# Layer 0 of a two-layer encoder: values of four head pairs by rows of tokens of a class, and eight reads of the head factors in place of sixteen

## The chip, the cores and the metric

The kernel runs on one core of one Trainium2 chip. The core has a matrix engine (TensorE, in the profile PE, its weight loads PEld), a vector engine (VectorE, DVE), a scalar engine (ScalarE, ACT), a general engine (GpSimd, POOL) and a queue engine (SyncE, SP) that issues nearly all DMAs here. Each engine works through its own instructions strictly in the order in which the program lists them; semaphores hold an instruction until what it needs is done.

The metric is the device time of one execution in microseconds (us). The kernel before takes 1204.83 us, the median of three runs from 1204.46 to 1208.03.

## The reference

One sequence of 512 tokens with 1024 features goes through two layers, each a token mixer and a squared-ReLU MLP with RMSNorm ahead of both. Layer 0, which the change touches, mixes by dilated sliding windows over 16 heads of 64 features:

```
A_GROUPS = ((128, 1, 6), (512, 4, 5), (2048, 16, 5))     # window, dilation, heads
qkv = xn @ w_qkv
...
lse = logsumexp(logits); p = exp(logits - lse); o = p @ v_sel
glses.append(logsumexp(lse over the group's heads) - log(nh))
alpha = softmax(stack(glses))                             # over the three groups
out = concat([o_g * (3 * alpha_g)]) @ w_o
```

Heads 0 to 5 look at 129 neighbours. Heads 6 to 15 look only at tokens whose number leaves the same remainder modulo 4, so for them the 512 tokens fall into four classes of 128 and a class attends to itself alone. Each head's output is scaled, token by token, by a factor that needs the sums of the softmax of all heads: 1 over the head's own sum times its group's weight.

## The kernel before, in words

**Layout and precision.** Activations lie turned: features on the 128 partitions, tokens along the free dimension, eight tiles of 128x512 for 1024 features. Every product of weights is made from a rounded part and a rest of both operands, three matmuls for each block of 128 features (helper `mm3`, lines 168 to 170 of the profile: high by high, high by low, low by high). The weights are the stationary operand and 512 tokens stream past. Weights come in units of 1 MB from a list (`units`), fetched one unit ahead into two buffers (`raw`, L154), rounded on ScalarE (`whi`, L157) and subtracted on VectorE (`wlo`, L158), each in two pieces. A unit's DMA can be issued only when the subtraction two units earlier has released the buffer.

**Layer 0's mixer.** Heads go in pairs (64 + 64 features make one tile of 128 partitions). For a pair: logits (L505), a bias and a minimum on VectorE (L485), exponentials and their sums on ScalarE (L487, two buffers `psg`), four transposes on TensorE (L538), a copy to SBUF on VectorE (L539). Then `values0(j)` makes the values of pairs 2j and 2j+1: 24 matmuls a pair, a multiplication by the norm's factor with the tokens sorted by class on VectorE (L550, `v`), four transposes on TensorE (L553), a copy on ScalarE (L555, `vn`), eight products with the probabilities (L565, into `o_ps`; the profile counts two records for each) and a copy (L567, `o`).

**The head factors.** `group_stats` sums the softmax sums by group. The sums of heads 6 to 15 are held by class, those of heads 0 to 5 by token, so each goes to DRAM and back in the other order: `exS` (L631) and `allN` (L632). `head_factors` makes the factors (`sA`, last step L602), `factors` turns them on TensorE (L642), copies them (`fT`, L644) and writes them to DRAM (`fac`, L645); heads 6 to 15 go first, heads 0 to 5 need `allN`. `spread` reads them back, each row repeated over 64 partitions (`fB`, L652): two DMAs for a pair of heads, sixteen in all.

**The output projection.** For each pair, in the order of `HEADS`, VectorE multiplies outputs and factors (L670), ScalarE rounds (`oh`, L678) and VectorE subtracts (`ol`, L679). Then eight tiles of 128 output features are made from four units of `a_w_o`, 24 matmuls for a tile, so 192 in all, and added to the residual `h` (L684).

**What sets the order.** A scheduler orders every engine's instructions when the program is built, from its own estimates. The code can move it with `high_priority` and with `issue_after`, which keeps what follows behind a named instruction. On the chip the order is fixed.

Of the kernel before, what the change touches and what calls it, by code (L numbers as in the profile page):

```python
# [11 lines left out]
F32 = mybir.dt.float32  # L12
# [70 lines left out]
def tile_encoder(ctx: ExitStack, tc: tile.TileContext, x, rel_bias, gains, norm_final_g,  # L83
# [15 lines left out]
    def acc_tile():  # L99
        return ps_acc.tile([P, 512], F32, tag="acc", name="acc")  # L100

    def s_tile():
        return ps_s.tile([P, 512], F32, tag="s", name="s_ps")
# [39 lines left out]
    def unit(w, r0, kt, c0, nc_):  # L143
        units.append((w, r0, kt, c0, nc_))
# [22 lines left out]
    def mm3(ps, ahi, alo, bhi, blo, first, last):  # L167
        nc.tensor.matmul(ps, ahi, bhi, start=first, stop=False)  # L168
        nc.tensor.matmul(ps, ahi, blo, start=False, stop=False)  # L169
        nc.tensor.matmul(ps, alo, bhi, start=False, stop=last)  # L170

    def linear_steps(ct0, kt, ncol, xs, on_out, bank=None, hooks=(), hold=None, order=None):

# [99 lines left out]
    def qkv_unit(w, part, j):  # L273
        unit(w, 0, KT, part * DM + j * 256, 256)
# [9 lines left out]
                    unit(mlp_w_out[i], c * 1024 + q * 512, 4, 0, 512)  # L284

    MLP_ORDER = [("in", 0), ("in", 1), ("out", 0), ("in", 2), ("out", 1), ("in", 3), ("out", 2), ("out", 3)]
    for part, j in ((0, 0), (1, 0), (0, 1), (1, 1), (2, 0), (0, 2), (1, 2), (2, 1), (0, 3), (1, 3), (2, 2), (2, 3)):
        qkv_unit(a_w_qkv, part, j)
    for c in range(4):
        unit(a_w_o, 0, KT, c * 256, 256)  # L290
    mlp_units(0)
# [101 lines left out]
    def lam():  # L393

        lam4 = spool.tile([P, 4, 64], F32, tag="nsq", name="lam4")
        nc.sync.dma_start(lam4.rearrange("p a b -> p (a b)"),
                          b_lambda.rearrange("a b -> (a b)").unsqueeze(0).broadcast_to([P, 256]))
        lprod = spool.tile([P, 2, 64], F32, tag="nsq", name="lprod")
        lsum = const.tile([P, 2], F32, name="lsum")
        nc.vector.tensor_mul(lprod, lam4[:, 0::2, :], lam4[:, 1::2, :])  # L400
        nc.vector.tensor_reduce(lsum, lprod, axis=AX.X, op=ALU.add)
        nc.scalar.activation(lsum, lsum, AF.Exp)
        nc.vector.tensor_sub(nlam, lsum[:, 1:2], lsum[:, 0:1])
        nc.vector.tensor_scalar(nlam, nlam, -LAMBDA_INIT, None, op0=ALU.add)
# [137 lines left out]
    def values0(j):  # L542
# [26 lines left out]

        run(linear_steps(2 * j, KT, 256, norm.xs, out_v))  # L570

    allN = l0p.tile([P, NB, 3, 2], F32, name="allN", bufs=1)
    allS = l0p.tile([P, NB, 3, 2], F32, name="allS", bufs=1)
    exN = dram.tile([SEQ, 2], F32, name="exN")
# [12 lines left out]
    def head_factors(al, parts):  # L587

        M = l0p.tile([P, NB, 1], F32, tag="fM", name="fM")
        nc.vector.tensor_reduce(M, al[:, :, :, 0], axis=AX.X, op=ALU.min)  # L590
        e = l0p.tile([P, NB, 3], F32, tag="fe", name="fe")
        nc.vector.tensor_sub(e, al[:, :, :, 0], M.broadcast_to([P, NB, 3]))
        nc.scalar.activation(e, e, AF.Exp, scale=-1.0)
        nc.vector.tensor_mul(e, e, al[:, :, :, 1])
        W = l0p.tile([P, NB, 1], F32, tag="fW", name="fW")
        nc.vector.tensor_reduce(W, e, axis=AX.X, op=ALU.add)
        nc.vector.reciprocal(W, W)
        nc.vector.tensor_scalar(W, W, 3.0, None, op0=ALU.mult)
        nc.vector.tensor_mul(e, e, W.broadcast_to([P, NB, 3]))
        for s, lo, hi, g in parts:  # L600
            nc.vector.reciprocal(s[:, :, lo:hi], s[:, :, lo:hi])
            nc.vector.tensor_mul(s[:, :, lo:hi], s[:, :, lo:hi], e[:, :, g:g + 1].broadcast_to([P, NB, hi - lo]))  # L602
# [11 lines left out]
        hankel(B1[:, 5:10, :], 11, 5, E_G2, P)  # L614
    values0(0)
    lam()
    probs0(2)
    probs0(3)
    group_stats(allN[:, :, 0, :], mnN, sN, 6)
# [18 lines left out]
    def factors(h0, h1):  # L638
        n = (h1 - h0) * NB
        with tc.high_priority():  # L640
            T = t_tile()
            nc.tensor.transpose(T[0:n, 0:P], sA[:, h0:h1, :].rearrange("p h b -> p (h b)"), ident)  # L642
            fT = l0p.tile([40, P], F32, tag="fT", name="fT")
            nc.scalar.copy(fT[0:n], T[0:n, 0:P])  # L644
        nc.sync.dma_start(fac[h0 * NB:h1 * NB], fT[0:n])  # L645

    def spread(*pairs):
        f = l0p.tile([P, 2, SEQ], F32, tag="ptn", name="fB", bufs=4)
        for i, p in enumerate(pairs):
            for hh, rows in enumerate((lo64, hi64)):  # L650
                a = fac[0:1, 0:1]
                nc.sync.dma_start(f[rows, i, :], bass.AP(tensor=a.tensor, offset=a.offset + (2 * p + hh) * SEQ,  # L652
                                                         ap=[[0, 64], [1, SEQ]]))
            F[p] = f[:, i, :]

    head_factors(allS, [(sS, 0, 5, 1), (sS, 5, 10, 2)])
    factors(6, 16)
    spread(3, 4)
    head_factors(allN, [(sN, 0, 6, 0)])
    factors(0, 6)  # L660
    spread(5, 0)
    spread(1, 2)
    spread(6, 7)
    values0(2)
    values0(3)

    oh_, ol_ = {}, {}
    HEADS = (3, 4, 5, 0, 1, 2, 6, 7)
    for p in HEADS:
        nc.vector.tensor_mul(F[p], O[p], F[p])  # L670
        hi = hpool.tile([P, SEQ], F32R, tag=f"Bh{p}", name=f"oh{p}")
# [15 lines left out]

    nm = Norm(G_MLP0, "A")
    on = residual(nm)
    for c in range(4):  # L690
        run(linear_steps(2 * c, KT, 256, (oh_, ol_), on, bank=wide, order=HEADS))
    l0.close()
    qk.close()
# [374 lines left out]
```

## Time and profile before

| | |
|---|---|
| median of the runs | 1204.83 us |
| profiled execution, its own time | 1205.12 us |
| its span | 1203.1 us |
| TensorE busy | 1186.0 us, 99% of the span |
| weight loads busy | 992.1 us, 82% |
| VectorE busy | 628.2 us, 52% |
| ScalarE busy | 501.1 us, 42% |
| GpSimd busy | 82.0 us, 7% |
| mean granted TensorE clock | 0.997 of full speed |

Times within the profile are us from the start of the span. The stage that the change touches runs from about 152 us (the first value product of pair 4) to 234 us (the last addition of the output projection). A row of the timeline gives start, length, engine, line, operation, what is written and read, and in brackets the idle time ahead of it with what ended it. TensorE's records overlap: a matmul of 512 columns is shown with 0.39 us while the next one starts 0.23 us after it.

### The profile page before, as it was taken

The page shows a single profiled execution, that of the slowest core. Times are in us where ns is not written, and L with a number is a line of the kernel's source. Part 1 is how long each engine was busy: PE and PEld are TensorE (multiplying, and loading weights), DVE is VectorE, ACT ScalarE, POOL GpSimd, SP SyncE. Part 2 cuts the span into 40 slices and gives each one's busy share as a digit, 9 for nine tenths or more (in the row PEclk, how much of TensorE's full clock was granted, in tenths as well). Part 3 has the DMA queues.
Part 4 walks back from the last instruction along what each step waited for, and adds up shares of the span by engine and source line. Part 5 has one row for each costly group of instructions (what it writes and reads, how often), then busy time and mean ns, then how long its engine had stood idle before and what let it go on. Part 6 is the DMA issues. An engine that isn't in the chain of part 4 may idle for free.

```text
span 1203.1 us, 14799 instructions
## 1 busy us (share of the span) xinstructions
PE 1186.0 (99%) x5888; PEld 992.1 (82%) x5888; DVE 628.2 (52%) x1056; ACT 501.1 (42%) x924; POOL 82.0 (7%) x141
## 2 busy tenths in 40 slices
PE   8999999999999999999999999999999999999997
PEld 6888877888888888888888898987888888888887
DVE  5875467544434334425458868675644344334323
ACT  6663345443323313313357666664443134223233
POOL 0000000200000000001101221222200000000012
PEclk9999999999999999999999999999999999999999
DMA  7622223323323332233423323312323332333211
GB/s 226 143 83 71 71 92 99 113 84 105 105 77 99 105 105 87 89 105 105 127 94 102 101 82 101 117 51 83 97 83 105 105 102 76 103 105 105 77 64 70
DMA packets 106827, 117.82 MB, mean 98 GB/s; under 512 B 5014, under 2 KB 97366, under 8 KB 106710
## 3 DMA queue, kind: packets, MB, share of 16 engines
q1 hardware_dynamic: 106694, 116.61, 30.7%
q8 instruction: 46, 0.75, 0.3%
q0 software_dynamic: 64, 0.27, 0.1%
q14 instruction: 23, 0.18, 0.0%
HBM read 114.60 MB, written 2.27 MB: 97 GB/s over the span
## 4 chain that ended last, share of the span: by engine, by line
PE 95%; DMA 2%; DVE 1%; issue 1%; SPq 0%; ACT 0%; POOLq 0%; POOL 0%; DVEq 0%; ACTq 0%
PE acc L169 15%; PE acc L168 15%; PE acc L170 15%; PE s_ps L168 14%; PE s_ps L170 14%; PE s_ps L169 14%; PE o_ps L915 2%; PE s_ps L358 1%; PE s_ps L359 1%; PE t_ps L906 1%; PE o_ps L565 1%; PE s_ps L505 0%; PE t_ps L527 0%; DMA fac<-fT 0%; DMA raw<-in_a_w_qkv_dram 0%
## 5 line engine op out<-in xcount | busy, mean ns | idle before, releaser
L157 ACT CAST whi<-raw 128x1024 fp32r<-128x1024 f32 (+1 forms) x196 | 189.1, 1014 | 385.6 <-PE s_ps L169 205.3
L158 DVE TENSOR_TENSOR wlo<-raw,whi 128x1024 fp32r<-128x1024 f32 (+1 forms) x196 | 223.4, 1180 | 38.4 <-ACT whi L157 37.9
L168 PE MATMUL acc<-Ah,whi 128*128 128x512 f32 x472 | 185.6, 393 | 0.0
L170 PE MATMUL acc<-Ah,wlo 128*128 128x512 f32 x472 | 185.5, 393 | 0.0
L169 PE MATMUL acc<-Al,whi 128*128 128x512 f32 x472 | 184.8, 392 | 0.0
L168 PE MATMUL s_ps<-Ah,whi 128*128 128x512 f32 x352 | 137.7, 393 | 0.6 <-ACT whi L330 0.6
L169 PE MATMUL s_ps<-Al,whi 128*128 128x512 f32 x352 | 137.3, 392 | 0.0
L170 PE MATMUL s_ps<-Ah,wlo 128*128 128x512 f32 x352 | 136.9, 392 | 0.0
L170 PEld LDWEIGHTS acc<-Ah,wlo 128*128 128x128 f32 x472 | 88.8, 188 | 18.4
L169 PEld LDWEIGHTS acc<-Al,whi 128*128 128x128 f32 x472 | 88.8, 188 | 18.1
L168 PEld LDWEIGHTS acc<-Ah,whi 128*128 128x128 f32 x472 | 88.8, 188 | 17.7
L713 ACT ACTIVATE u<-u 128x512 f32<-128x512 f32 x64 | 40.0, 628 | 96.6 <-DVE u L712 96.6
L168 PEld LDWEIGHTS s_ps<-Ah,whi 128*128 128x128 f32 x352 | 66.3, 189 | 16.3 <-ACT whi L330 1.4
L722 DVE TENSOR_TENSOR h<-h,s_ps 128x512 f32<-128x512 f32 x33 | 22.7, 688 | 108.0 <-PE s_ps L170 108.0
L170 PEld LDWEIGHTS s_ps<-Ah,wlo 128*128 128x128 f32 x352 | 66.5, 189 | 13.8
L169 PEld LDWEIGHTS s_ps<-Al,whi 128*128 128x128 f32 x352 | 66.5, 189 | 13.7
L712 DVE SCALAR_TENSOR_TENSOR u<-s_ps,rB 128x512 f32<-128x512 f32 x38 | 26.3, 691 | 76.0 <-PE s_ps L170 73.8
L245 POOL TENSOR_TENSOR nacc<-nacc,nsq 128x512 f32<-128x512 f32 x18 | 25.9, 1438 | 534.2 <-ACT nsq L243 533.7
L168 PE MATMUL s_ps<-Bh,whi 128*128 128x512 f32 x152 | 59.1, 389 | 0.0
L169 PE MATMUL s_ps<-Bl,whi 128*128 128x512 f32 x152 | 59.1, 389 | 0.0
L170 PE MATMUL s_ps<-Bh,wlo 128*128 128x512 f32 x152 | 59.1, 389 | 0.0
L887 DVE CUSTOM_DVE_ANT_0 p<-s_ps,bias 128x512 f32<-128x512 f32 x64 | 43.3, 688 | 26.3 <-PE s_ps L359 17.7
(246 smaller groups left out, 2148.2 us busy)
## 6 DMA issues: line engine op xcount, KB each, us to landing
raw<-in_mlp_w_in_dram SPq DMA_DIRECT2D x32, 1024.0 KB, 5.3
raw<-in_mlp_w_out_dram SPq DMA_DIRECT2D x32, 1024.0 KB, 5.2
raw<-in_b_w_qkv_dram SPq DMA_DIRECT2D x12, 1024.0 KB, 5.2
raw<-in_a_w_qkv_dram SPq DMA_DIRECT2D x10, 1024.0 KB, 6.6
bias<-fd SPq DMA_DIRECT2D x16, 448.0 KB, 3.4
raw<-in_a_w_o_dram SPq DMA_DIRECT2D x4, 1024.0 KB, 5.2
raw<-in_b_w_o_dram SPq DMA_DIRECT2D x4, 1024.0 KB, 6.3
h<-in_x_dram SPq DMA_DIRECT2D x8, 256.0 KB, 4.4
```

The source lines that it names most:

```text
L157: nc.scalar.copy(hi[:, :, c], raw[:, :, c])
L158: nc.vector.tensor_sub(lo[:, :, c], raw[:, :, c], f32(hi[:, :, c]))
L168: nc.tensor.matmul(ps, ahi, bhi, start=first, stop=False)
L169: nc.tensor.matmul(ps, ahi, blo, start=False, stop=False)
L170: nc.tensor.matmul(ps, alo, bhi, start=False, stop=last)
L245: eng.tensor_add(self.acc, self.acc, sq)
L358: nc.tensor.matmul(S, q[m][:, qs], k[m][:, ks], start=True, stop=False)
L712: nc.vector.scalar_tensor_tensor(u, ps, 0.0, nm.rB, op0=ALU.max, op1=ALU.mult)
L713: nc.scalar.activation(u, u, AF.Square)
L722: nc.vector.tensor_add(hT[ct], hT[ct], ps)
L887: nc.vector.tensor_tensor_reduce(out=xt, in0=S, in1=bias[h][m][:, b * P:b * P + SEQ], scale=1.0, scalar=3.0e38, op0=ALU.add, op1=ALU.min, ...
L915: marks["PV"] = nc.tensor.matmul(O[:, b, :], aT[:, k, :], v[:, k, es], start=k == 0, stop=k == NB - 1)
```

## The change

**Values.** Pairs 0 to 3 are done as before. For pairs 4 to 7 a new function `values_by_class` takes `values0(2)` and `values0(3)`'s place. The normalised activations are now the stationary operand, for each class the 128 tokens of it, that is every fourth column of the tile, and the weights of the four pairs (512 columns) stream past. So the values come with tokens on the partitions, one PSUM bank for each class, and need no transposes. The norm's factor is then one number for each partition; it is written to DRAM and read back by class once, early (`exR`, `rC`), and applied by ScalarE when it copies a bank (`vc`). The weights come as two units of 512 features by 512 columns. The matmuls of one half of the features run over all four banks, then those of the other half. The eight products of a pair with the probabilities are as many as before; they go to `o_ps` and `t_ps` banks in turn.

**Factors.** `spread` reads the factors of two pairs with one DMA for each half of the partitions, 64 x 2 x 512 elements in place of 64 x 512; eight DMAs move what sixteen moved. The pairs go together as (3,4), (6,7), (0,1), (2,5).

**Order.** The fourth bank of the first half is kept behind the turning of the factors of heads 6 to 15, the second bank of the second half behind that of heads 0 to 5. `HEADS` runs from 0 to 7. The first unit of the projection is written out with its two tiles going side by side, pair by pair.

```diff
-    for part, j in ((0, 0), (1, 0), (0, 1), (1, 1), (2, 0), (0, 2), (1, 2), (2, 1), (0, 3), (1, 3), (2, 2), (2, 3)):
+    for part, j in ((0, 0), (1, 0), (0, 1), (1, 1), (2, 0), (0, 2), (1, 2), (2, 1), (0, 3), (1, 3)):
         qkv_unit(a_w_qkv, part, j)
+    for half in range(2):
+        unit(a_w_qkv, half * 512, 4, 2 * DM + 512, 512)
...
+    exR = dram.tile([SEQ, 1], F32, name="exR")
+    rC = l0p.tile([P, NB, 1], F32, name="rC", bufs=1)
+
+    def values_by_class(behind):
+        xh, xl = norm.xs
+        v = [qkp.tile([P, SEQ], F32, tag=tag, name="vc", bufs=3) for tag in ("q0", "k0", "q0", "k0")]
+        banks = [acc_tile(), acc_tile(), s_tile(), s_tile()]
+        mark = None
+        for half in range(2):
+            hi, lo = next_w()
+            for c, ps in enumerate(banks):
+                mark = behind.get((half, c), mark)
+                with tc.issue_after(mark.ins) if mark else nullcontext():
+                    for k in range(4):
+                        d = 4 * half + k
+                        ah, al = (t.rearrange("p (m c) -> p c m", c=4)[:, c, :] for t in (xh[d], xl[d]))
+                        mm3(ps, ah, al, hi[:, k, :], lo[:, k, :], d == 0, d == KT - 1)
+                if half == 1:
+                    nc.scalar.activation(v[c], ps, AF.Copy, scale=rC[:, c, :])
+        for p in range(4, 8):
+            ops = (o_tile, t_tile, t_tile, o_tile)[p - 4]()
+            for b in range(NB):
+                for hh, rows in enumerate((lo64, hi64)):
+                    e = (p - 4) * P + 64 * hh
+                    nc.tensor.matmul(ops[rows, b * P:(b + 1) * P], v[3 - b][:, e:e + 64], PT[2 * p + hh][:, b, :],
+                                     start=True, stop=True)
+            o = hpool.tile([P, SEQ], F32, tag=f"Bl{p}", name=f"o{p}")
+            nc.scalar.copy(o, ops)
+            O[p] = o
...
     lam()
+    nc.sync.dma_start(exR.rearrange("(q p) s -> p q s", p=P), norm.r.unsqueeze(2))
+    nc.sync.dma_start(rC, exR.rearrange("(m c) s -> m c s", c=4))
...
-    def spread(*pairs):
+    def spread(p0, p1):
         f = l0p.tile([P, 2, SEQ], F32, tag="ptn", name="fB", bufs=4)
-        for i, p in enumerate(pairs):
-            for hh, rows in enumerate((lo64, hi64)):
-                a = fac[0:1, 0:1]
-                nc.sync.dma_start(f[rows, i, :], bass.AP(tensor=a.tensor, offset=a.offset + (2 * p + hh) * SEQ,
-                                                         ap=[[0, 64], [1, SEQ]]))
-            F[p] = f[:, i, :]
+        for hh, rows in enumerate((lo64, hi64)):
+            a = fac[0:1, 0:1]
+            nc.sync.dma_start(f[rows], bass.AP(tensor=a.tensor, offset=a.offset + (2 * p0 + hh) * SEQ,
+                                               ap=[[0, 64], [2 * (p1 - p0) * SEQ, 2], [1, SEQ]]))
+        F[p0], F[p1] = f[:, 0, :], f[:, 1, :]
...
-    factors(6, 16)
+    turned_s = factors(6, 16)
     spread(3, 4)
+    spread(6, 7)
     head_factors(allN, [(sN, 0, 6, 0)])
-    factors(0, 6)
-    spread(5, 0)
-    spread(1, 2)
-    spread(6, 7)
-    values0(2)
-    values0(3)
+    turned_n = factors(0, 6)
+    spread(0, 1)
+    spread(2, 5)
+    values_by_class({(0, 3): turned_s, (1, 1): turned_n})
...
-    HEADS = (3, 4, 5, 0, 1, 2, 6, 7)
+    HEADS = (0, 1, 2, 3, 4, 5, 6, 7)
...
-    for c in range(4):
+    hi, lo = next_w()
+    banks = [wide(), wide()]
+    for p in HEADS:
+        for c, ps in enumerate(banks):
+            s = slice(c * P, (c + 1) * P)
+            mm3(ps, hi[:, p, s], lo[:, p, s], oh_[p], ol_[p], p == HEADS[0], p == HEADS[-1])
+    for c, ps in enumerate(banks):
+        on(c, ps)
+    for c in range(1, 4):
         run(linear_steps(2 * c, KT, 256, (oh_, ol_), on, bank=wide, order=HEADS))
```

**How it moves instructions.** Line numbers in the changed kernel are higher: the turning of the factors is L679 there (L642 before), the write of `fac` L682 (L645), the read of `fB` L690 (L652), the products with the probabilities L601 (L565), the multiplication by the factors L707 (L670), the subtraction for `ol` L716 (L679).

On SP, around the factors, before:

```order
L154 DMA raw<-in_a_w_o_dram 128x8x256 x2
L631 DMA exS<-allS 512x1x4
L632 DMA allN<-exS 128x4x4
L154 DMA raw<-in_a_w_o_dram 128x8x256
L645 DMA fac<-fT 40x128
L645 DMA fac<-fT 24x128
L652 DMA fB<-fac 64x512 x16
L154 DMA raw<-in_a_w_o_dram 128x8x256
```

and in the changed kernel:

```order
L154 DMA raw<-in_a_w_o_dram 128x8x256 x2
L668 DMA exS<-allS 512x1x4
L669 DMA allN<-exS 128x4x4
L682 DMA fac<-fT 40x128
L690 DMA fB<-fac 64x2x512 x4
L682 DMA fac<-fT 24x128
L154 DMA raw<-in_a_w_o_dram 128x8x256
L690 DMA fB<-fac 64x2x512 x4
L154 DMA raw<-in_a_w_o_dram 128x8x256
```

The third unit of `a_w_o` stood ahead of both writes of `fac`; now it stands behind them and ahead of the last four reads, which bring the factors of pairs 0, 1, 2 and 5.

On VectorE, behind the factors of heads 0 to 5 (`o_1229`, `o_803`, `o_857` and `o_1184` are the outputs of pairs 3, 0, 1 and 2, `o_1757` that of pair 4; `ol_1794` belongs to pair 0, `ol_1799` to pair 1), in the changed kernel:

```order
L637 TENSOR_TENSOR sA<-sA,fe 128x4x6
L707 TENSOR_TENSOR fB<-o_1229,fB 128x512
L158 TENSOR_TENSOR wlo<-raw,whi 128x8x128 x2
L707 TENSOR_TENSOR fB<-o_803,fB 128x512
L707 TENSOR_TENSOR fB<-o_857,fB 128x512
L707 TENSOR_TENSOR fB<-o_1184,fB 128x512
L158 TENSOR_TENSOR wlo<-raw,whi 128x8x128 x2
L716 TENSOR_TENSOR ol_1794<-fB,oh_1793 128x512
L707 TENSOR_TENSOR fB<-o_1757,fB 128x512
L716 TENSOR_TENSOR ol_1799<-fB,oh_1798 128x512
```

Before, the subtractions for `v` stood among these, and only one unit's `wlo` stood here, behind six of the eight multiplications. Now the first unit's `wlo`, whose end lets SP issue the third unit, stands behind the multiplication of pair 3, and the second unit's stands ahead of the first `ol`.

On TensorE, around the first turning of factors, in the changed kernel (`wlo` and `whi` now stream; the `s_ps` below L679 is the fourth bank):

```order
L168 MATMUL s_ps<-whi,Ah_122 128x512
L169 MATMUL s_ps<-wlo,Ah_122 128x512
L170 MATMUL s_ps<-whi,Al_130 128x512
L540 MATMUL t_ps<-ident,psg 128x128 x4
L679 MATMUL t_ps<-ident,sA 40x128
L168 MATMUL s_ps<-whi,Ah_119 128x512
L169 MATMUL s_ps<-wlo,Ah_119 128x512
```

Before, this turning stood 68 value products into the stage; now it stands 36 in, and the second one (24x128) 60 in.

More of the change, by code (lines that the diff above doesn't have):

```diff
@@ L169, in mm3 @@
         nc.tensor.matmul(ps, ahi, blo, start=False, stop=False)
-        nc.tensor.matmul(ps, alo, bhi, start=False, stop=last)
+        return nc.tensor.matmul(ps, alo, bhi, start=False, stop=last)
     def linear_steps(ct0, kt, ncol, xs, on_out, bank=None, hooks=(), hold=None, order=None):
@@ L641, in factors @@
             T = t_tile()
-            nc.tensor.transpose(T[0:n, 0:P], sA[:, h0:h1, :].rearrange("p h b -> p (h b)"), ident)
+            mark = nc.tensor.transpose(T[0:n, 0:P], sA[:, h0:h1, :].rearrange("p h b -> p (h b)"), ident)
             fT = l0p.tile([40, P], F32, tag="fT", name="fT")
@@ L645, in factors @@
         nc.sync.dma_start(fac[h0 * NB:h1 * NB], fT[0:n])
-    def spread(*pairs):
+        return mark
+    def spread(p0, p1):
         f = l0p.tile([P, 2, SEQ], F32, tag="ptn", name="fB", bufs=4)
-        for i, p in enumerate(pairs):
-            for hh, rows in enumerate((lo64, hi64)):
-                a = fac[0:1, 0:1]
-                nc.sync.dma_start(f[rows, i, :], bass.AP(tensor=a.tensor, offset=a.offset + (2 * p + hh) * SEQ,
-                                                         ap=[[0, 64], [1, SEQ]]))
-            F[p] = f[:, i, :]
+        for hh, rows in enumerate((lo64, hi64)):
[3 more added lines that the diff above has]
+        F[p0], F[p1] = f[:, 0, :], f[:, 1, :]
     head_factors(allS, [(sS, 0, 5, 1), (sS, 5, 10, 2)])
-    factors(6, 16)
+    turned_s = factors(6, 16)
     spread(3, 4)
+    spread(6, 7)
     head_factors(allN, [(sN, 0, 6, 0)])
-    factors(0, 6)
-    spread(5, 0)
-    spread(1, 2)
-    spread(6, 7)
-    values0(2)
-    values0(3)
+    turned_n = factors(0, 6)
+    spread(0, 1)
+    spread(2, 5)
+    values_by_class({(0, 3): turned_s, (1, 1): turned_n})
     oh_, ol_ = {}, {}
-    HEADS = (3, 4, 5, 0, 1, 2, 6, 7)
+    HEADS = (0, 1, 2, 3, 4, 5, 6, 7)
     for p in HEADS:
```

## The prediction

> **What bounds the kernel now.** I read the page first: its busy shares and the chain that ended last.
>
> ```profile
> PE 1186.0 (99%) x5888; PEld 992.1 (82%) x5888; DVE 628.2 (52%) x1056; ACT 501.1 (42%) x924; POOL 82.0 (7%) x141
> PE 95%; DMA 2%; DVE 1%; issue 1%; SPq 0%; ACT 0%; POOLq 0%; POOL 0%; DVEq 0%; ACTq 0%
> ```
>
> TensorE is the bound, and what it can still save is work taken off it or a hole closed. The chain's 2% of DMA is worth a look: for a while something other than TensorE ends last. The timeline of TensorE in the stage that changes shows where:
>
> ```profile
> 151.86 0.39 PE L168 MATMUL acc<-Ah,whi 128*128 128x512 f32 x1
> 152.09 0.40 PE L169 MATMUL acc<-Al,whi 128*128 128x512 f32 x1
> ...
> 157.45 1.16 PE L505 MATMUL s_ps<-k,q 64*128 64x128 f32 x16
> ...
> 172.58 0.27 PE L642 MATMUL t_ps<-ident,sA 128*24 128x128 f32 x1 [0.92 <-DVE sA L602]
> 172.68 0.60 PE L553 MATMUL t_ps<-ident,v 128*128 128x128 f32 x4
> 173.96 1.09 PE L565 MATMUL o_ps<-pt,vn 128*64 128x128 f32 x16 [0.68 <-ACT vn L555]
> ...
> 180.60 1.09 PE L565 MATMUL o_ps<-pt,vn 128*64 128x128 f32 x16
> 181.62 0.66 PE L553 MATMUL t_ps<-ident,v 128*128 128x128 f32 x4
> 182.04 0.48 PE L169 MATMUL acc<-Al,whi 128*128 128x512 f32 x1
> ...
> 183.40 0.50 PE L168 MATMUL s_ps<-oh,whi 128*128 128x512 f32 x1 [0.65 <-ACT oh L678]
> ...
> 186.33 1.12 PE L553 MATMUL t_ps<-ident,v 128*128 128x128 f32 x4 [2.20 <-DVE v L550]
> 187.38 1.98 PE L565 MATMUL o_ps<-pt,vn 128*64 128x128 f32 x16
> ...
> 189.68 0.40 PE L169 MATMUL s_ps<-ol,whi 128*128 128x512 f32 x1
> ```
>
> Four holes in brackets, 4.45 us. Behind the last one the same work is slower (1.98 us against 1.09 for eight products, 1.12 against 0.66 for four transposes): the granted clock was halved there.
>
> ```profile
> 186.00:189.40 3.40, 3.07 (x21) 2.41 (x21) 3.40 (x6) 2.76 (x5) 0.00 (x0) 0.50 0.42 131
> ```
>
> That is another 1.35 us. And each set of four transposes of `v` holds the stream 0.42 us (181.62 to 182.04) to 0.6, four sets together 2.0. So the old scheme costs at most 7.8 us.
>
> **What the change takes away.** The 16 transposes, 2.0 us. Also the four copies `vn` and VectorE's four multiplications `v`, and with them the two holes that name them (0.68 and 2.20). The value products stay 96 of 512 columns, the products with the probabilities 32, the projection 192: moved, at one price.
>
> **The strided weight load.** A weight load now takes every fourth column. No stationary operand of before is so spread, so I bound it. These are matmuls of 256 columns in layer 1, and the cast to `oh`, whose output has a step of four elements for pairs 3 to 7 and of one for pairs 0 to 2.
>
> ```profile
> 695.56 0.28 PE L168 MATMUL acc<-whi,Ah 128*128 128x256 f32 x1
> 695.67 0.28 PE L169 MATMUL acc<-wlo,Ah 128*128 128x256 f32 x1
> 695.79 0.28 PE L170 MATMUL acc<-whi,Al 128*128 128x256 f32 x1
> L170 PEld LDWEIGHTS acc<-Ah,wlo 128*128 128x128 f32 x472 | 88.8, 188 | 18.4
> L678 ACT CAST oh<-fB x8: 618/1144/1183, 182.2 to 195.8; 128x512 fp32r<-128x512 f32 x8
> ```
>
> Loads of 128 columns follow each other every 0.12 us there, so one occupies its path 0.12 us at most, though its record has 188 ns. Under a 512-column matmul (0.23 us from start to start) it has 0.11 us to spare. ScalarE pays 1183/618 = 1.9 times for the step of four. 1.9 x 0.12 = 0.23 us: just hidden. Lower bound nothing; upper bound 1.9 times the whole record, 0.36 us, or 0.13 us more for each of 96 products. I take nothing, as the nearest row for a load's pace is the 256-column one.
>
> [...] By an estimate with a factor of 2 on the 0.12 us, 0.24, the sum would change by less than 1 us; a larger factor is the second rival.
>
> **The chain that takes over.** With the transposes gone, what TensorE waits for next are the factors. SP's timeline and the landing times (for the write `exS`, for `fB`, for a weight unit `raw`):
>
> ```profile
> 164.30 0.59 SPq L631 DMA_DIRECT2D exS<-allS  x1
> 167.71 0.37 SPq L632 DMA_DIRECT2D allN<-exS  x1
> 170.87 0.37 SPq L154 DMA_DIRECT2D raw<-in_a_w_o_dram  x1
> 171.34 2.12 SPq L645 DMA_DIRECT2D fac<-fT  x2
> 176.27 10.33 SPq L652 DMA_DIRECT2D fB<-fac  x16
> DMA to landing us min/median/max: 3.4/3.4/3.4
> DMA to landing us min/median/max: 2.8/3.0/3.5
> DMA to landing us min/median/max: 5.0/5.2/5.4
> L652 SPq DMA_DIRECT2D fB<-fac x16: 449/590/599, 176.3 to 186.0; - x16
> ```
>
> and VectorE's rows that the steps below use:
>
> ```profile
> 164.17 0.11 DVE L585 TENSOR_SCALAR allS<-gsz 128x4 f32<-128x4 f32 x1
> 164.91 0.69 DVE L539 COPY pt<-t_ps 128x512 f32<-128x512 f32 x1
> 165.92 0.29 DVE L602 TENSOR_TENSOR sA<-sA,fe 128x20 f32<-128x20 f32 x2
> 169.54 0.17 DVE L590 TENSOR_REDUCE fM<-allN 128x4 f32<-128x12 f32 x1 [1.26 <-DMA allN<-exS]
> 169.62 1.22 DVE L158 TENSOR_TENSOR wlo<-raw,whi 128x1024 fp32r<-128x1024 f32 x1
> 172.23 0.20 DVE L602 TENSOR_TENSOR sA<-sA,fe 128x24 f32<-128x24 f32 x1
> L670 DVE TENSOR_TENSOR fB<-o,fB x8: 674/694/701, 179.8 to 195.1; 128x512 f32<-128x512 f32 x8
> L679 DVE TENSOR_TENSOR ol<-fB,oh x8: 672/1115/1149, 186.7 to 197.0; 128x512 fp32r<-128x512 f32 x8
> 188.91 2.37 DVE L158 TENSOR_TENSOR wlo<-raw,whi 128x1024 fp32r<-128x1024 f32 x2
> ```
>
> Now step by step, on the clock of before.
>
> 1. The last logits stand 12 products into the stage, not 23, so 2.5 us earlier (151.86 + 12 x 0.23 + two transposes, 154.8). Little of it arrives: the last head's exponentials wait for one of two `psg` buffers, which the transposes of the head before it free between value products (about 160.9), and VectorE copies the last turned head (0.69) ahead of the last sum. I get `exS` issued at 164.0, before 164.3.
> 2. The factors of heads 6 to 15 need 1.4 us more (164.17 to 166.2, less the copy): 165.4. TensorE is at their turning after 36 products, 163.0. **New hole, 2.4 us**, and every value product behind it waits. The second turning stands 24 products later, 171.0; its factors come at 171.2, since the `wlo` of 1.22 us is gone from between 169.54 and 172.23. Hole 0.2.
> 3. TensorE ends the value products at 179.3, waits for the last bank's copy (the hole of 0.68 for `vn` again, 0.75), and makes three sets of products, 3 x 1.02, to 183.2. Next stands the first product with `oh` of pair 0.
> 4. When is that there? `exS` lands at 164.0 + 3.4 = 167.4; SP issues the read of `allN` and at 167.8 `fac`. No weight unit stands ahead of that write; before, one issued 0.47 us ahead of it did, and the first `fB` came 4.9 us after `fac`. I take 3.0 (bounds 1.8, from 167.71 to 169.54, and 4.9): 170.8. Four `fB` at 0.59 each; the first two, with twice the data (1 MB takes 2.2 us more than 128 KB, so 0.3), land by 174.8.
> 5. VectorE multiplies pair 3 (0.69), then subtracts the first unit (2.37): 177.9. Only then can SP issue the third unit, and the reads for pairs 0, 1, 2 and 5 are queued behind it. 177.9 + 5.2 = 183.1 for the unit, then four reads of 256 KB at 0.6: pair 0 and 1 at 184.4, pair 2 and 5 at 185.6.
> 6. `oh` of pair 0 is ready at 184.4 + 0.69 + 0.62 = 185.7. **Hole 2.5 us.** Four products and the last set of eight take TensorE to 187.7.
> 7. `ol` of pair 0 stands on VectorE behind the multiplications of pairs 0 to 2 (to 186.3) and the second unit's subtraction (2.37): 188.7 + 0.67 = 189.4. **Hole 1.8 us**; TensorE goes on at 189.5. From there VectorE needs 1.8 us for a pair (0.69 + 1.12) against 2.7 for its twelve products, so nothing more waits.
>
> **The sum.** At 189.5 four of the 192 projection products and all others are done. Before, at 189.68, three were done and one set of eight, 1.02 us, still to come. So the change is ahead by 0.2 + 0.23 + 1.0 = **1.4 us**. Beyond that both have the same products, and before ran them without a hole to the last addition:
>
> ```profile
> 233.97 0.69 DVE L684 TENSOR_TENSOR h<-h,s_ps 128x512 f32<-128x512 f32 x1 [3.21 <-PE s_ps L170]
> ```
>
> (189.68 + 189 x 0.227 + 1.02 = 233.6; 0.23 is the step of the rows above, 0.227 the mean that fits this run.) Counted the other way, 7.8 of old cost less new holes of 2.4 + 0.2 + 0.75 + 2.5 + 1.8 = 7.65 leaves 0.15 ahead; the list of old costs misses what a switch between kinds of products loses without a hole. I take the sum by times and keep 1 us of doubt. The two early DMAs for `rC` move SP's weight loads of that stage by about a microsecond; TensorE waits for none there. If that cover were gone it would cost that microsecond.
>
> The profiled execution took 1205.12 us (span 1203.1, 2.0 around it), 0.3 above the median of 1204.83. So: 1204.83 - 1.4 = **1203.4 us**, within 0.3% (3.6 us), which is about what a measurement of this kernel tells from no change.
>
> **Rivals.** *The chain does not gate: faster.* If the reads of step 5 come early (a quicker `fac`, or reads that pass the weight unit), holes 6 and 7 close and TensorE is through at 185.2 in place of 189.5: 4.3 us more, 1199.1 us. For it: every step is a landing time that I carried over. Against: the order of SP and VectorE is fixed, and `fac` before waited just as I assume. Chance 0.23.
>
> *The strided load is not hidden: slower.* At 0.36 us for each value product the 36 ahead of step 2 cost 4.7 us, which the chain of the factors carries along, and the 60 others 7.8. TensorE then ends the values at 191.8 and reaches the state of step 7 at 197.5 in place of 189.5: 8.0 less 1.4, 1211.4 us. It decides from 0.04 us more for a product: 36 x 0.04 = 1.4, the whole gain. For it: the cast's 1.9. Against: 0.11 us to spare. [...] Chance 0.17.
>
> *The half clock comes back behind a new hole.* Before, the holes of 0.65 and 2.20 within 3.6 us brought it; steps 6 and 7 leave 2.5 and 1.8 within 6.3, step 2 has 2.4. It would cost up to 1.7 us, after 189.5 only, since before that TensorE waits anyway: 1205.1, still no change.
>
> That eight reads are not half of sixteen is certain: each moves twice the bytes; the queue saves eight issues of 0.59 us, which are hidden behind step 5's unit.
>
> **Numbers.** Chain gates, 0.60 (half clock included): 1203.4, by itself 1201.5 to 1206. Not gating 0.23, load not hidden 0.17. Range 1199.3 to 1208.0: it takes in most of the first rival and the middle of the second. Faster by over 0.3%: 0.24; within: 0.59; slower: 0.17.
>
> **What would show it.** Right: a hole of 2 us or more ahead of the first turning of factors, two more between the third and the last set of products and the first `ol`, `fB` of pair 0 landing after the third unit of `a_w_o`, and 0.23 us between value products. Wrong: value products at over 0.25 us; no hole after the third set of products; or a hole beyond 190 us, where VectorE would be the bound.

## The result and the profile after

The changed kernel is slower: 1215.07 us median (1213.41 to 1216.91) against 1205.76 us of the kernel before on the same chip. The ratio is 1.0082, with a 95% interval of 1.0069 to 1.0095. The profiled execution has a span of 1211.3 us against 1203.1, so 8.2 us are to be found between the two traces.

I looked first at two marks that both kernels have: the last set of logits but one, ahead of the stage that was changed, and the last row shown in the prediction, an addition to `h` at the end of that stage (233.97 us before). Of before, and then of the changed kernel:

```profile
150.43 1.16 PE L505 MATMUL s_ps<-k,q 64*128 64x128 f32 x16
```

```profile
157.64 1.16 PE L507 MATMUL s_ps<-k,q 64*128 64x128 f32 x16
...
242.25 0.69 DVE L721 TENSOR_TENSOR h<-h,s_ps 128x512 f32<-128x512 f32 x1 [3.21 <-PE s_ps L170]
```

7.21 us are lost before the stage of the values begins, where no instruction of TensorE was changed. The stage itself takes 84.61 us in place of 83.54, another 1.07. So the question is what happens ahead of 150 us, and there the change puts only the two small DMAs for `rC`. SP's timeline, of before:

```profile
31.78 0.88 SPq L434 DMA_DIRECT2D B<-fd  x2
37.08 0.37 SPq L154 DMA_DIRECT2D raw<-in_a_w_qkv_dram  x1
...
40.73 39.20 SPq L154 DMA_DIRECT2D raw<-in_a_w_qkv_dram  x4
```

The same place in the changed kernel:

```profile
30.79 0.88 SPq L436 DMA_DIRECT2D B<-fd  x2
32.37 0.36 SPq L652 DMA_DIRECT2D exR<-rstd  x1
43.59 0.34 SPq L653 DMA_DIRECT2D rC<-exR  x1
44.05 0.37 SPq L154 DMA_DIRECT2D raw<-in_a_w_qkv_dram  x1
...
47.55 39.57 SPq L154 DMA_DIRECT2D raw<-in_a_w_qkv_dram  x4
```

and the row on it in the list of SP's waits, whose columns are the sum in us, how often, and the longest:

```profile
SPq L653 <- DMA exR<-rstd: 10.8, 1, 10.8
```

Issuing the two takes 0.7 us. But the second one reads what the first one writes, so SP holds it until `exR` has landed, 10.8 us, and everything behind it in SP's order is held too. The weight unit goes out at 44.05 in place of 37.08, and the next one at 47.55 in place of 40.73. That next one lands 19.5 us after its issue (19.7 before), so it is late by about as much as it was issued late. ScalarE's cast of it, in the kernel before, with the exponentials that follow:

```profile
60.52 2.00 ACT L157 CAST whi<-raw 128x1024 fp32r<-128x1024 f32 x2 [0.81 <-DMA raw<-in_a_w_qkv_dram]
...
64.49 0.51 ACT L487 ACTIVATE PN<-xt,mnN 128x256 f32<-128x256 f32 x1
```

and in the changed kernel, with what stands behind it on ScalarE and then on TensorE:

```profile
67.13 1.99 ACT L157 CAST whi<-raw 128x1024 fp32r<-128x1024 f32 x2 [8.00 <-DMA raw<-in_a_w_qkv_dram]
...
71.07 0.51 ACT L489 ACTIVATE PN<-xt,mnN 128x256 f32<-128x256 f32 x1
...
71.72 1.13 PE L529 MATMUL t_ps<-ident,PN 128*128 128x128 f32 x4 [7.30 <-ACT PN L489]
```

The stretch behind that, with the busy time of each engine and then the granted clock (0.54):

```profile
72.00:76.00 4.00, 4.00 (x14) 3.19 (x14) 3.84 (x15) 3.47 (x15) 0.00 (x0) 0.54 0.74 249
```

ScalarE stands 8 us before a cast whose data are not there. Three more casts and then the exponentials `PN` are queued behind it, and TensorE waits 7.30 us for those. When it goes on, the clock is halved for most of 4 us. In the kernel before, the same four transposes wait for nothing:

```profile
66.40 0.60 PE L527 MATMUL t_ps<-ident,PN 128*128 128x128 f32 x4
```

71.72 - 66.40 = 5.3 us of the 7.21 are their delay, and the half clock accounts for most of the rest. The cast is 6.6 us late and the transposes only 5.3, because before, the exponentials had been ready 1.3 us ahead of TensorE: that was all the cover there was. The hole is longer than the delay, because this execution came to it 2 us ahead. It was ahead by that much already where SP writes `fd` (27.00 us against 29.14), in front of anything that the change touches; of the kernels below, some write it at 27 us and some at 29. TensorE's wait names ScalarE; only ScalarE's own wait names the DMA, and only SP's wait tells why that DMA was late.

In the stage of the values the holes are where they were looked for (TensorE's timeline of the changed kernel):

```profile
173.94 0.27 PE L679 MATMUL t_ps<-ident,sA 128*40 128x128 f32 x1 [2.30 <-DVE sA L637]
...
190.99 1.09 PE L601 MATMUL o_ps<-pt,vc 128*64 128x128 f32 x16 [0.78 <-ACT vc L595]
...
195.31 0.50 PE L168 MATMUL s_ps<-oh,whi 128*128 128x512 f32 x1 [1.48 <-ACT oh L715]
...
199.30 0.50 PE L169 MATMUL s_ps<-ol,whi 128*128 128x512 f32 x1 [1.77 <-DVE ol L716]
```

and the clock behind the first of them is 0.50:

```profile
175.00:178.00 3.00, 3.00 (x8) 2.34 (x7) 0.25 (x2) 0.00 (x0) 0.00 (x0) 0.50 0.12 10
```

Less 7.21, the four holes end at 166.7, 183.8, 188.1 and 192.1 on the clock of before.

### The profile page after: what moved, and what is told of

Read it like the earlier page. It is cut to its first block, busy times and chain, and to the rows that moved or that the text cites. A ratio compares the mean times of both kernels' runs of the same rounds, so it can differ in the third digit from the quotient of the medians.

```text
span 1211.3 us, 14749 instructions
## 1 busy us (share of the span) xinstructions
PE 1185.3 (98%) x5872; PEld 996.1 (82%) x5872; DVE 624.1 (52%) x1052; ACT 501.6 (41%) x924; POOL 82.3 (7%) x141
## 4 chain that ended last, share of the span: by engine, by line
PE 94%; DMA 4%; DVE 1%; issue 1%; ACT 0%; SPq 0%; POOLq 0%; POOL 0%; DVEq 0%; ACTq 0%
PE acc L169 14%; PE acc L170 14%; PE acc L168 14%; PE s_ps L168 14%; PE s_ps L169 14%; PE s_ps L170 14%; PE o_ps L961 2%; DMA raw<-in_a_w_qkv_dram 2%; PE s_ps L360 1%; PE s_ps L361 1%; PE t_ps L952 1%; DMA fB<-fac 1%; DVE wlo L158 1%; PE o_ps L567 1%; PE s_ps L507 0%
## 5 line engine op out<-in xcount | busy, mean ns | idle before, releaser
L168 PE MATMUL acc<-Ah,whi 128*128 128x512 f32 x440 | 172.9, 393 | 0.0
L170 PE MATMUL acc<-Ah,wlo 128*128 128x512 f32 x440 | 172.9, 393 | 0.0
L169 PE MATMUL acc<-Al,whi 128*128 128x512 f32 x440 | 172.4, 392 | 0.0
L169 PEld LDWEIGHTS acc<-Al,whi 128*128 128x128 f32 x440 | 83.1, 189 | 17.0
L170 PEld LDWEIGHTS acc<-Ah,wlo 128*128 128x128 f32 x440 | 83.0, 189 | 17.0
L168 PEld LDWEIGHTS acc<-Ah,whi 128*128 128x128 f32 x440 | 83.0, 189 | 16.6
```

The lines of the kernel that those rows point to most:

```text
L170: return nc.tensor.matmul(ps, alo, bhi, start=False, stop=last)
```

## Experiments

Two theories stood against each other. **Theory 1**: the read of `rC` holds SP's queue, and with it the weights. **Theory 2**, the prediction's own account: these DMAs are harmless, and whatever is lost is lost in the values.

**The two DMAs alone, in the kernel before.**

```diff
 values0(0)
 lam()
+nc.sync.dma_start(exR.rearrange("(q p) s -> p q s", p=P), norm.r.unsqueeze(2))
+nc.sync.dma_start(rC, exR.rearrange("(m c) s -> m c s", c=4))
 probs0(2)
...
```

> The kernel before with only the two small DMAs added: the write of exR and the read of rC, at the place where the changed kernel has them; rC is used by nothing, the values still come by transposes. Theory 1 (SyncE's queue): the read of rC can issue only when exR has landed, 10.8 us after its own turn comes in the changed kernel's trace, and the weight unit behind it (issued at 44.05 there, at 37.08 before) is late by 7 us, and TensorE with it. Then this kernel is some 7 us slower than before, 1212 to 1214 us, with a hole of about 7 us on TensorE between 64 and 72 us and a stretch of half clock behind it. Theory 2 (the prediction's): the two DMAs cost at most a microsecond and the time is lost between 152 and 234 us, in the values. Then 1205 to 1207 us.

1214.47 us against 1205.9; ratio 1.0068 (1.0049 to 1.0086). Its row in SP's waits:

```profile
SPq L620 <- DMA exR<-rstd: 11.0, 1, 11.0
```

and in TensorE's timeline:

```profile
72.21 1.12 PE L527 MATMUL t_ps<-ident,PN 128*128 128x128 f32 x4 [7.96 <-ACT PN L487]
```

A write and a read of 2 KB that nothing uses cost about as much as the whole change. Theory 2 falls.

**The read of `rC` later.**

```diff
 nc.sync.dma_start(exR.rearrange("(q p) s -> p q s", p=P), norm.r.unsqueeze(2))
-nc.sync.dma_start(rC, exR.rearrange("(m c) s -> m c s", c=4))
...
-nc.sync.dma_start(allS[:, :, 0, :], exN.rearrange("(m c) s -> m c s", c=4))
+seen = nc.sync.dma_start(allS[:, :, 0, :], exN.rearrange("(m c) s -> m c s", c=4))
+with tc.issue_after(seen.ins):
+    nc.sync.dma_start(rC, exR.rearrange("(m c) s -> m c s", c=4))
```

> The changed kernel with the read of rC moved behind the read of allS on SyncE (about 95 us in the trace), where exR has long landed and rC is still 80 us early; the write of exR stays. Theory 1 (the wait for exR's landing holds the weights): 7.2 us of the loss go, 1215.1 - 7.2 = 1207.9 us (1206 to 1209), the hole of 7.30 us ahead of the transposes of line 529 goes with the half clock behind it, and the stage of the values keeps its own four holes (2.30, 0.78, 1.48, 1.77). Theory 2 (the values): no change, 1215 us. A third possibility, that the write itself and not the read's wait disturbs the queue: part of the 7.2 us stays.

1206.58 us against 1205.9; ratio 1.0001 (0.9992 to 1.001). SP's timeline:

```profile
33.66 0.36 SPq L652 DMA_DIRECT2D exR<-rstd  x1
37.02 0.37 SPq L154 DMA_DIRECT2D raw<-in_a_w_qkv_dram  x1
...
87.75 0.60 SPq L659 DMA_DIRECT2D rC<-exR  x1
```

and the two marks:

```profile
150.46 1.16 PE L507 MATMUL s_ps<-k,q 64*128 64x128 f32 x16
...
235.50 0.69 DVE L722 TENSOR_TENSOR h<-h,s_ps 128x512 f32<-128x512 f32 x1 [3.21 <-PE s_ps L170]
```

The write stays where it was and disturbs nothing; only the read's place has moved. The weight unit is out at 37.02 and the first mark at 150.46, as before. Theory 1 holds. What is left is the change proper: its stage takes 85.04 us against 83.54 in these two traces (one execution each), and the times of the two kernels can't be told apart.

**Why `exR` took 10.8 us to land.** Two causes were possible: the two reads of `B` issued just ahead of it, or the write itself. First both DMAs were put where no `B` is in flight:

```diff
-nc.sync.dma_start(exR.rearrange("(q p) s -> p q s", p=P), norm.r.unsqueeze(2))
...
 seen = nc.sync.dma_start(allS[:, :, 0, :], exN.rearrange("(m c) s -> m c s", c=4))
 with tc.issue_after(seen.ins):
+    nc.sync.dma_start(exR.rearrange("(q p) s -> p q s", p=P), norm.r.unsqueeze(2))
     nc.sync.dma_start(rC, exR.rearrange("(m c) s -> m c s", c=4))
```

> The changed kernel with both small DMAs, the write of exR and the read of rC, behind the read of allS (about 88 us), where no reads of B are in flight. What it asks: why exR took 10.8 us to land in the changed kernel. If it was the two reads of B issued 1.6 us ahead of it (their packets run to 38.26 us), the read of rC here can issue about 4 us after the write, as allS does after exN (3.4 to 3.9). If 512 elements of 4 bytes are slow by themselves, it waits 7 us or more. The time is that of e2_rc_late (1206.6 us) either way, within a microsecond, since SyncE issues no weight unit until 97.7 us there.

1207.13 us, ratio 1.0012 (0.9995 to 1.0029). Then the same with each factor written twice, which makes the elements 8 bytes:

```diff
-exR = dram.tile([SEQ, 1], F32, name="exR")
+exR = dram.tile([SEQ, 2], F32, name="exR")
...
+nc.gpsimd.tensor_copy(r2, norm.r.unsqueeze(2).broadcast_to([P, NB, 2]))
...
-    nc.sync.dma_start(exR.rearrange("(q p) s -> p q s", p=P), norm.r.unsqueeze(2))
+    nc.sync.dma_start(exR.rearrange("(q p) s -> p q s", p=P), r2)
```

> The kernel e13_both_late with exR and rC two words wide: each token's factor is written twice (a copy on GpSimd makes the pair, far ahead), so the 512 elements of the write are 8 bytes each, as exN's, in place of 4. Everything else is the same. The wait of the read of rC for exR's landing was 10.1 us with 4 bytes, that of the read behind exN 4.0 us with 8. If the element's size is the reason, the wait is 3 to 4.5 us here; if it is something else of this DMA (its place, its queue), 10 us stay.

1207.72 us, ratio 1.0022 (1.0008 to 1.0036). SP's waits in the first, with the neighbouring write of 8-byte elements, and then in the second:

```profile
SPq L659 <- DMA exR<-rstd: 10.1, 1, 10.1
SPq L656 <- DMA exN<-allN: 4.0, 1, 4.0
```

```profile
SPq L661 <- DMA exR<-r: 4.0, 1, 4.0
SPq L658 <- DMA exN<-allN: 3.9, 1, 3.9
```

512 elements of 4 bytes keep the reader waiting 10.1 us, with only the small read of `allS` issued ahead of them; 512 elements of 8 bytes at the same place, twice the data, 4.0. At its first place the 8-byte version (the same edit in the changed kernel) does less:

> The changed kernel, with the two DMAs where it has them (about 32 us), but elements of 8 bytes in place of 4. The wait of the read for the write was 10.8 us there. If the element's size is all of it, 4 us, SyncE issues the weight unit at 37 us as before, and the loss is gone: 1207 us. If the reads of B ahead of it in the queue (packets until 38.3 us) hold it as well, it lands some 3 us after those packets, at 41 us: a wait of 8.5 us, the weight unit at 41.5 in place of 44, and 2 to 3 us of the 7.2 back: 1212.5 us.

1213.99 us, ratio 1.0076 (1.0054 to 1.0097), and the wait is

```profile
SPq L655 <- DMA exR<-r: 7.3, 1, 7.3
```

so both causes are there, though they don't add up. Behind the reads of `B` the small elements take 10.8 us and the larger 7.3; away from them 10.1 and 4.0. For the 4 bytes of the changed kernel the size of the element alone makes nearly the whole wait. The median is 1.1 us below the changed kernel's, which the two intervals don't tell from nothing, and I had expected 2 to 3. The unit that TensorE waits for was issued at 44.76 us in place of 47.55 but landed 22.8 us after its issue in place of 19.5; why it took longer isn't shown. The cure is not to wait there at all.

**The strided weight load.** The kernel with the late read, its `x` taken by 128 neighbouring columns; the tokens of a bank are then others, so the values aren't those of the reference.

```diff
-ah, al = (t.rearrange("p (m c) -> p c m", c=4)[:, c, :] for t in (xh[d], xl[d]))
+ah, al = (t[:, c * P:(c + 1) * P] for t in (xh[d], xl[d]))
```

> The kernel e2_rc_late with each class's 128 columns of x taken side by side (columns c*128 to c*128+127) in place of every fourth one: the weight load of the 96 value products reads contiguous data, everything else is the same; the output is then not the reference's, since the tokens of a bank are other ones. The value products stand 0.235 us apart in the changed kernel and projection products 0.227. If the stride is the reason, 0.227 here and TensorE through the values 0.8 us earlier (96 x 0.0085); if it is something else in these products (the weights as the moving side), 0.235 stays. The time: if the chain of factors sets the end of the stage, at most 0.8 us less than e2_rc_late, more likely 0 to 0.5. If the stride cost what the prediction's rival says (0.36 us a product), the spacing would have shown it already.

1207.88 us, ratio 1.0014 (1.0001 to 1.0027): not faster than the kernel with the late read, against what I expected, though the values themselves are. One of the groups of weight loads (busy us, mean ns), strided and then side by side:

```profile
L168 PEld LDWEIGHTS acc<-whi,Ah 128*128 128x128 f32 x16 | 5.0, 310 | 0.1
```

```profile
L168 PEld LDWEIGHTS acc<-whi,Ah 128*128 128x128 f32 x16 | 3.0, 188 | 0.5
```

A piece of TensorE's timeline that begins right behind a transpose, strided:

```profile
159.34 0.60 PE L168 MATMUL s_ps<-whi,Ah 128*128 128x512 f32 x1
159.78 0.40 PE L169 MATMUL s_ps<-wlo,Ah 128*128 128x512 f32 x1
160.02 0.40 PE L170 MATMUL s_ps<-whi,Al 128*128 128x512 f32 x1
```

and side by side, with the hole that follows later:

```profile
159.47 0.48 PE L168 MATMUL s_ps<-whi,Ah 128*128 128x512 f32 x1
159.79 0.39 PE L169 MATMUL s_ps<-wlo,Ah 128*128 128x512 f32 x1
160.02 0.40 PE L170 MATMUL s_ps<-whi,Al 128*128 128x512 f32 x1
...
188.30 0.50 PE L168 MATMUL s_ps<-oh,whi 128*128 128x512 f32 x1 [4.41 <-ACT oh L716]
```

and a stretch soon after that hole, with the clock at 0.50:

```profile
192.60:196.00 3.40, 3.40 (x9) 2.64 (x8) 3.40 (x6) 2.75 (x3) 0.00 (x0) 0.50 0.88 300
```

The load takes 310 ns in place of 188. Under a product of 512 columns most of that is hidden: 0.235 us from one product to the next on average against 0.227 to 0.231. Behind a short transpose it is not: the first product takes 0.44 us to the next one, against 0.32. TensorE is through the values 3.1 us sooner after its first mark (about 1.5 of it because no half clock fell there: 10 products from 167.46 to 171.34 with the stride, 3.9 us in place of 2.35), and then stands 4.41 us ahead of `oh` where it stood 1.51. The half clock fell behind that hole, onto projection products that wait for nothing, where it does cost: by an estimate from the row above, 1.7 of its 3.4 us. So in this kernel the end of the stage is set by the chain of the factors and not by TensorE's work.

That the half clock fell elsewhere is not the stride's doing. The kernel with both small DMAs late has the stride, and in this stage the same instructions as the kernel with the late read. Of the kernel with the late read, whose first turning waits 2.31 us, and then of the one with both late (clock third from the right; first turning 2.30 us):

```profile
167.80:171.00 3.20, 3.20 (x9) 2.53 (x8) 0.34 (x2) 0.21 (x1) 0.00 (x0) 0.51 0.11 9
```

```profile
167.80:171.00 3.20, 3.20 (x15) 3.20 (x15) 0.34 (x2) 0.12 (x2) 0.00 (x0) 1.00 0.11 9
...
188.43 0.50 PE L168 MATMUL s_ps<-oh,whi 128*128 128x512 f32 x1 [3.27 <-ACT oh L716]
...
190.00:196.00 6.00, 4.61 (x20) 3.53 (x17) 6.00 (x9) 4.92 (x7) 0.00 (x0) 0.50 0.49 165
```

It went through the values 1.5 us sooner, `oh` came no sooner (188.43 against 188.15), and the half clock came behind that hole. Its stage takes 86.96 us, and that of the 8-byte version of it, with half clock at both places, 87.61, against 85.04. So one trace of this stage is good to some 2.5 us only, unless the half clock falls at the same place. Against the 86.96, where the half clock fell at the same place, neighbouring columns (86.10) make the stage 0.9 us shorter; the times don't show it.

**The reads of the factors ahead of the third unit.** The kernel with the late read, and SP's order changed at one point.

```diff
+        with tc.issue_after(hold.pop().ins) if hold else nullcontext():
-        fetched.append(nc.sync.dma_start(raw, ...))
+            fetched.append(nc.sync.dma_start(raw, ...))
...
-    spread(2, 5)
+    last_read = spread(2, 5)      # spread now returns its last DMA
...
+    hold.append(last_read)        # the next unit fetched is the third of a_w_o
     for c in range(1, 4):
```

> The kernel e2_rc_late with the reads of the factors of pairs 0, 1, 2 and 5 issued ahead of the third unit of a_w_o on SyncE; the orders of the other engines are the same. Theory A (steps 5 to 7 of the prediction: the wait of the third unit for VectorE holds the reads, and they hold oh and ol): fB of pair 0 lands about 4 us earlier, the holes of 1.48 us (ahead of the first product with oh) and 1.77 us (ahead of the first with ol) close, and the kernel is 2.5 to 3.3 us faster than e2_rc_late, about 1204.7 us. Theory B (the holes are set by TensorE's late start into the values and by VectorE's subtractions, not by the reads): less than 1 us.

1202.59 us against 1205.9; ratio 0.9967 (0.9953 to 0.998): faster than the kernel before, and 4.0 us faster than with the late read alone. Where VectorE multiplies pair 0, with the late read alone:

```profile
186.71 1.29 DVE L708 TENSOR_TENSOR fB<-o,fB 128x512 f32<-128x512 f32 x2 [8.11 <-DMA fB<-fac]
```

and with the reads first (SP's four reads and the unit behind them, VectorE, TensorE):

```profile
176.57 2.52 SPq L692 DMA_DIRECT2D fB<-fac  x4
179.20 8.20 SPq L155 DMA_DIRECT2D raw<-in_a_w_o_dram  x2
...
181.77 1.29 DVE L710 TENSOR_TENSOR fB<-o,fB 128x512 f32<-128x512 f32 x2 [4.78 <-DMA fB<-fac]
...
187.63 0.50 PE L170 MATMUL s_ps<-ol,whi 128*128 128x512 f32 x1 [0.35 <-DVE ol L719]
```

The hole ahead of `oh` is gone and the one ahead of `ol` is 0.35. Theory A of that run holds in the main: the third unit held the reads. Its wait for VectorE is the smaller part: counted from the first mark the reads were issued 1.1 us sooner and pair 0 was multiplied 3.4 us sooner, and the rest is the unit's own megabyte, no longer ahead of them (the slowest of the eight reads of `fB` lands in 5.4 us in place of 7.7). Between the two marks the stage takes 81.63 us, 3.4 less than with the late read, with the half clock behind the first turning in both. (In this execution the first mark stands 1.5 us earlier as well. It was ahead already at the write of `fd`, 26.91 us against 29.08, in front of all that was edited, so 3.4 is the better figure for the edit.)

**What bounds the stage then.** Two edits of the kernel with the reads first move the turnings of the factors.

```diff
-values_by_class({(0, 3): turned_s, (1, 1): turned_n})
+values_by_class({(1, 0): turned_s, (1, 2): turned_n})     # later
+values_by_class({(0, 3): turned_s, (1, 0): turned_n})     # or: the second one earlier
```

> The kernel e8_reads_first with the two turnings of the factors put 12 value products later each: the first behind half 0 of the values in place of ahead of its last bank, the second 12 products after it would stand. What it asks: with the reads no longer held by the third unit, is the hole of 2.30 us ahead of the first turning, with the 1.4 us of half clock behind it (166.5 to 169.8 us), still paid for? Theory A (TensorE's own length through the values now sets the end): the first turning waits for nothing, the half clock goes, the second turning comes about 1 us earlier, and the kernel gains 1 to 2.5 us, 1200.1 to 1201.6 us. Theory B (the chain from the second turning over fac and the reads to oh still sets the end): the hole comes back ahead of the first product with oh or ol, and the gain is under 1 us (the second turning's own shift).

> The kernel e8_reads_first with only the second turning moved, 12 value products earlier (right behind half 0). The factors of heads 0 to 5 are ready at 170.8 us there and TensorE would reach the turning at about 169.9: a hole of about 1 us that was not there. Theory A (TensorE's own length sets the end): slower by about 1 us, 1203.6 us. Theory B (the chain from the second turning sets the end): fac is written about 1.9 us earlier, the hole of 0.35 ahead of ol closes, and no more than 0.4 us is gained, 1202.2 us.

Later: 1204.23 us against 1205.12, ratio 0.9987 (0.9974 to 0.9999). The hole of 2.30 and the half clock are gone, and TensorE waits elsewhere instead:

```profile
183.89 0.50 PE L169 MATMUL s_ps<-oh,whi 128*128 128x512 f32 x1 [0.92 <-ACT oh L718]
...
188.34 0.50 PE L170 MATMUL s_ps<-ol,whi 128*128 128x512 f32 x1 [2.22 <-DVE ol L719]
```

The stage gets 0.57 us shorter (81.06 between the marks), and the times show no gain over the kernel with the reads first; that is theory B. The second one earlier: 1203.92 us, ratio 0.9984 (0.9973 to 0.9995), the stage 83.67 us, 2.0 longer, with a hole of 2.59 us ahead of that turning where I had expected about 1 (no half clock fell behind the first turning, so TensorE came sooner). So the two limits lie close together once the reads go first: the 3.45 us by which TensorE is sooner through the values in the first variant bring 0.57, and the 2.45 by which it is later in the second cost 2.0. That rests on one trace of each; the times of the two can't be told apart.

## Why the prediction was wrong

**The step that failed** stands at the end of the sum: "The two early DMAs for `rC` move SP's weight loads of that stage by about a microsecond; TensorE waits for none there." I priced the two by their issue. The price is the wait of a read for the landing of what it reads: 10.8 us on an ordered queue, 7.0 us on the weight unit, 7.30 us as a hole, 7.21 us at the end. Two things were wrong: a wait was left out, and it was three times as long as its nearest row. The row that could have told me of the wait is in the trace of before: such a pair of DMAs, the write of `exN` and the read of `allS`, at 83.70 and 87.79 us, where SP's waits of the kernel before say

```profile
SPq L621 <- DMA exN<-allN: 3.6, 1, 3.6
```

That row alone would not have saved the forecast. With 3.6 us for the landing, SP in the kernel with the late read, which writes `exR` at 33.66, would have issued the unit at 38.1 (33.66 + 0.36 + 3.6, and 0.46 for the read) in place of 37.02. That is about the microsecond that I gave, and TensorE had 1.3 us of cover there. What made it 10.8 is the 4-byte element and the reads of `B` ahead of it, and no row of the prediction shows a write of either kind. No rival asked what such a write costs, because the step stood far from the stage that I looked at.

The steps of the stage itself can be read on the kernel with the late read, which stands on the clock of before (150.46 against 150.43):

| Step | Predicted | Measured |
|---|---|---|
| 1: `exS` issued | 164.0 | 165.3 |
| 2: hole ahead of the first turning | 2.4 | 2.31 |
| 2: hole ahead of the second | 0.2 | none |
| 3: value products end | 179.3 | 183.0 |
| 3: hole for the last bank's copy | 0.75 | 0.78 |
| 4: `fac` written | 167.8 | 169.0 |
| 5: third unit issued | 177.9 | 178.6 |
| 6: pair 0 multiplied from | 184.4 | 186.7 |
| 6: hole ahead of `oh` | 2.5 | 1.51 |
| 7: hole ahead of `ol` | 1.8 | 2.17 |
| 7: TensorE goes on | 189.5 | 192.5 |

But for the second hole, of 0.2 us, the mechanism was right in each of them: which engine waits for whom, and in what order. Two terms were too small. The weight load behind a transpose is not hidden (0.12 us each, at eight places ahead of step 2), which I had priced at nothing for all 96 products; with neighbouring columns `exS` is issued at 164.56, 0.4 of which is that trace's own shift, so within 0.2 of my 164.0. And in step 5 I gave each read of 256 KB the 0.6 us between two issues; behind a full unit the two reads of pairs 0 and 1 were there 8.1 us after the unit's issue and not 6.5. The half clock behind the first turning adds 1.5 to the end of the value products, and the waits behind it take it in, as the kernel with both DMAs late shows. Together these make my -1.4 into +1.5 us between the marks, and 1206.58 us in the times: no change, and inside the range. Without the step that failed the time would have lain where I put it, but that is owed to the width of the range: the gain of 1.4 us did not come, and the stage was missed by 3 us.

**The rivals.** "The chain does not gate" was priced at 4.3 us below the forecast. The chain gates; with its reads let past the unit, 3.4 us were gained between the marks and 4.0 in the medians. "The strided load is not hidden" was priced at 1211.4 and its number lies nearer to the result than mine, but not its mechanism: products stand 0.235 us apart, not 0.36. From product to product my estimate with a factor of 2 on the 0.12 us was met: 0.235 us, or 0.8 us for all 96. The loads behind transposes, which it left out, cost about another microsecond (0.12 us at each of eight places). "The half clock comes back" happened twice in the changed kernel, behind the 7.30 us hole and behind the first turning. It did not come at steps 6 and 7, where I had priced it, but in the kernel with both DMAs late it did, and there the stage is 1.9 us longer than with the late read.

**What would have shown it.** All signs named for the stage came: the hole of over 2 us, two more ahead of `oh` and `ol`, the late reads, products at under 0.25 us, no hole behind that of `ol`. That last one ends at 192.1 on the clock of before, past the 190 us that I had named as a sign of being wrong; it is step 7, late, and no new bound. None of the signs looked ahead of 150 us, so all could come true in a kernel that is 9 us slower.

## What to carry to other kernels

In these runs a DMA that read back what another had just written held its queue for the whole landing time of the write (2.8 us for `exS`, 3.4 to 4.0 for `exN`, 4.0 to 11.0 for `exR`), and everything behind it as well (a weight unit by 7.0 us); put such a read where the queue has nothing to issue, or far behind its write, however small it is. Follow a change's every instruction to the place where it is issued, not only the stage that it is for: two marks at either end of the stage tell at once whether the time was lost inside it. And when a chain of small transfers bounds a stage, look first for what they are queued behind: here one weight unit, not needed yet, was worth 3.4 us of the stage, while faster products brought nothing that the times show. And read one trace of a stage with care where the clock can drop: the same work took 85.0 us and 87.0.

## What the runs showed of the hardware

- A write to DRAM of 512 elements of 4 bytes kept the reader waiting 10.1 us, with one small read issued ahead of it; with 8 bytes an element the same write, at the same place, took 4.0. Why 4 bytes are so slow isn't settled: only the sizes 4 and 8 were tried.
- A weight load of every fourth fp32 column takes 310 ns in place of 188. It adds up to 0.008 us to a product of 512 columns that follows another one, and 0.12 us to one that follows a transpose of 128 columns.
- The half clock (0.50 to 0.54 granted in the stretches shown) does not follow from a hole's length alone. Behind the hole of 2.30 or 2.31 us ahead of the first turning it came in the changed kernel, with the late read, with the reads first and in both 8-byte versions; it did not come with neighbouring columns, with both DMAs late and with the second turning earlier. It also came behind holes of 7.30 us (ahead of the transposes), of 4.41 and 3.27 (ahead of `oh`) and of 2.59 (second turning), and not behind 0.92 and 2.22 in the variant with both turnings later. Behind the 7.30 it cost time in full (about 1.9 of the 7.21 us); at the first turning the waits that follow took it in (`oh` at 188.43 us without it there, 188.15 with it). What decides whether the clock drops wasn't tried.
